# A hybrid decoder layer on one core: mask transfers of the SSD branch issued two groups ahead, with five wide buffers for three, and ScalarE's mask work in unbound halves

## The chip, the cores and the metric

The kernel runs on one core of a Trainium2 chip. A core has a matrix engine (TensorE, PE in the profile, its weight loads PEld), VectorE (DVE), ScalarE (ACT), GpSimd (POOL) and a sync engine (SP). Each engine works off its own instruction list in order; between engines there are semaphores. Transfers run on 16 DMA engines and are issued here from SP (weights) and POOL (masks). The metric is the device time of one execution in microseconds (us); lower is better. What is compared is the median of several executions.

## The reference, cut to what matters

The layer is a SwiGLU feed-forward, a mixer with two branches (Mamba-2 SSD and retention), and a second feed-forward, for 256 tokens of width 1024 in float32. The change touches the SSD branch: 4 groups of 8 heads, two chunks of 128 tokens.

```python
def segsum_exp(a):
    cs = jnp.cumsum(a, axis=-1)
    diff = cs[..., :, None] - cs[..., None, :]
    n = a.shape[-1]
    mask = jnp.tril(jnp.ones((n, n), dtype=bool))
    return jnp.exp(jnp.where(mask, diff, -jnp.inf))
...
    cb = jnp.einsum('bclgn,bcsgn->bgcls', cm, bm)
    scores = cb[:, :, None] * segsum_exp(a)
    y_diag = jnp.einsum('bgrcls,bcsgrp->bclgrp', scores, xdt)
...
    y_off = jnp.einsum('bclgn,cbgrpn,bgrcl->bclgrp', cm, prev_states, jnp.exp(a_cs))
    y = y_diag + y_off + xs * d_skip.reshape(g_, r_)[..., None]
```

`segsum_exp` is the decay mask: for every head a 128 x 128 matrix exp(cs[l] - cs[s]) for s <= l.

## The kernel before

**Weights and PE.** All projections run in split precision. A weight tile comes in by a transfer of 1 MB into `wst` (4 buffers). `half` makes of each half of it a rounded high part `wh` with a cast on ScalarE (L129) and the rest `wl` with a subtraction on VectorE (L130), 4 buffers each. `mm3` (L138 to L140) then runs three matmuls a product: high by high, high by low, low by high. So every weight tile needs two casts and two subtractions ahead of its 48 matmuls, and a late cast stops PE.

**Order of the work.** The mixer's steps are written out by hand in `ORDER`. A scheduler places each engine's instructions at build time: of those whose data it expects to be there, the one that stands first in the program goes first, so that later work can fill gaps. It works with expected times; the chip then runs each engine's list in order and waits where data are late. `tc.issue_after(ins)` binds what is issued inside it to stand behind the instruction `ins` on the same engine. `half` keeps its last cast and its last subtraction for that purpose (`last_hi`, `last_lo`).

**The SSD steps of a group g.** `decays` writes the cumulative sums of the decays to a small tensor `rows` in DRAM. `ml.g` (`mask_rows`) issues on POOL four transfers out of it: for both chunks the 8 heads' rows, broadcast to 128 partitions, into the wide buffers `m` (L645, 512 KB each), and two of 128 KB into `ec` (L648). `masks.g` (`ssd_masks`) does on ScalarE, for each chunk, eight Relus with the head's own sum as bias (L661) and an Exp (L170), then an Exp of `ec`. `bc` makes the score products of all groups, `mul.g` multiplies both masks by them on VectorE (L669), `states.g` scales the inputs (`xd` L626, `xe` L631) and makes the chunk's states on PE (L636), and `back.g` runs PE's products with the masks (L679) and the states (L689), and adds on VectorE (L685, L691, L692). `norma.g`, `normb.g` normalise, `z.g.*` are gate projections (their Silu at L170), `v.*` the retention's values, `bs.g.*` the branch's output projection.

**Buffers.** The wide buffers (tag `m`) are three: one group takes two. The first `m` tiles of the tag go to `dt` and `decays`, and retention later uses the same tag. `ec` has one buffer. In `ORDER`, `ml.g` stands behind `back.(g-1)`, the step that reads the former group's masks. ScalarE also switches its function table (`need`) between Exp ("e") and Silu ("s").

Of the kernel before, what the change touches and what calls it, by code (L numbers as in the profile page):

```python
# [12 lines left out]
F32 = mybir.dt.float32  # L13
F32R = mybir.dt.float32r
I32 = mybir.dt.int32
AF = mybir.ActivationFunctionType
ALU = mybir.AluOpType

P = 128
# [23 lines left out]
STAGE_BUFS = 4  # L43
HALF_BUFS = 4
SLOTS = 17
WIDE_BUFS = 3
F1 = 7

ORDER = (
# [30 lines left out]
def layer(ctx: ExitStack, tc: tile.TileContext, a, out, packing):  # L80
    nc = tc.nc
    pe, act, dve = nc.tensor, nc.scalar, nc.vector
# [10 lines left out]
    def nm(s):  # L93
        uid[0] += 1
        return f"{s}_{uid[0]}"
# [22 lines left out]
              .transpose(1, 0, 2))  # L118
        return st.rearrange("p (k n) -> p k n", k=nk)

    last_lo, last_hi = [None], [None]

    def half(v):
        nk, n = v.shape[1], v.shape[2]
        hi = wp.tile([P, 1024], F32R, tag="wh", name=nm("wh"), bufs=HALF_BUFS)
        lo = wp.tile([P, 1024], F32R, tag="wl", name=nm("wl"), bufs=HALF_BUFS)
        hi = hi[:, :nk * n].rearrange("p (k n) -> p k n", k=nk)
        lo = lo[:, :nk * n].rearrange("p (k n) -> p k n", k=nk)
        last_hi[0] = act.copy(hi, v).ins  # L129
        last_lo[0] = dve.tensor_tensor(lo, v, hi.bitcast(F32), ALU.subtract).ins  # L130
        return hi, lo

    def split_into(hi, lo, src):
# [34 lines left out]
    def lookup(*args, **kw):  # L168
        with tc.issue_after(phase["load"]):
            phase["uses"].append(act.activation(*args, **kw).ins)  # L170
# [89 lines left out]
    def early_project(w, cols, u, at_kt, between):  # L260
        sts = [load(w, 0, KD, c0, 256) for c0 in cols]
        ps = [proj_ps().rearrange("p f t -> p (f t)") for _ in range(2)]
        ps += [misc_ps() for _ in range(2)]
        for kh in range(2):
            hv = [half(st[:, 4 * kh:4 * kh + 4, :]) for st in sts]
            for kk in range(4):
                kt = 4 * kh + kk
                if kt == at_kt:
                    between()
                for i in range(2):  # L270
                    for f in range(2):
                        mm3(ps[2 * i + f][:, :T + 2], at(hv[i], al, kk, slice(f * P, (f + 1) * P)),
                            wide_at(u, kt), kt == 0, kt == KD - 1)
        return ps

    def pair_project(w, c0, u):
        st = load(w, 0, KD, c0, 256)
        ps = proj_ps()
        for f in range(2):
            hv = half(st[:, :, f * P:(f + 1) * P])  # L280
            for kt in range(KD):
                mm3(ps[:, f, :], at(hv, al, kt), at(u, al, kt), kt == 0, kt == KD - 1)
        return ps

    def split_project(w, c0, c1, u):
        st = stage()
        fetch(st, w, lambda m: np.stack([m[:, c:c + P].reshape(KD, P, P) for c in (c0, c1)])
              .transpose(2, 0, 1, 3))
        st = st.rearrange("p (j k n) -> p j k n", j=2, k=KD)
        ps = proj_ps()  # L290
        for f in range(2):
            hv = half(st[:, f])
            for kt in range(KD):
                mm3(ps[:, f, :], at(hv, al, kt), at(u, al, kt), kt == 0, kt == KD - 1)
        return ps
# [183 lines left out]
    with tc.tile_pool(name="mx", bufs=1, reuse_waits="tile") as mx:  # L479
# [6 lines left out]
        def small(shape, tag, bufs=1):  # L486
            return mx.tile(shape, F32, tag=tag, name=nm(tag), bufs=bufs)

        def wide(shape, dt=F32):
            return mx.tile(shape, dt, tag="m", name=nm("m"), bufs=WIDE_BUFS)  # L490

# [25 lines left out]
        def need(t):  # L517
            if now[0] != t:
                now[0] = t
                table(table_of[t])  # L520

        dt, av = small([P, 2, NH], "dt"), small([P, 2, NH], "av")
# [45 lines left out]
        def silu_half(key, c0, p2):  # L568
            need("s")
            if p2 == 0:  # L570
                zs[key] = slot([P, 4, T])
            if key == ("z", 0):
                for f in range(4):
                    lookup(zs[key][:, f, :], first[f][0], AF.Silu, bias=first[f][1])
                return
            ps = pair_project(w_in, c0 + p2 * 256, u)
            lookup(zs[key][:, 2 * p2:2 * p2 + 2, :], ps, AF.Silu)

        bn = small([P, 4, P], "bn")
        cs, dend = small([P, 2, NH], "cs"), small([P, NH], "dend")  # L580
        cbs, states, masks = [], {}, {}
# [56 lines left out]
            states[g] = xd, st  # L638

        def mask_rows(g):  # L640
            ec = small([P, 512], "ec")
            m = [wide([P, 8, P]) for _ in range(2)]
            masks[g] = ec, m
            for c in range(2):
                nc.gpsimd.dma_start(m[c], rows[c:c + 1, 8 * g:8 * g + 8, :].broadcast_to([P, 8, P]))  # L645
            for hh in range(2):
                src = rows[1:2, 8 * g:8 * g + 8, :].rearrange("o (i two) l -> two o i l", two=2)[hh]
                nc.gpsimd.dma_start(ec[hh * 64:hh * 64 + 64, :].rearrange("p (i l) -> p i l", i=4),  # L648
                                    src.broadcast_to([64, 4, P]))

        def ssd_masks(g):
            need("e")
            ec, m = masks[g]
            with tc.issue_after(last_hi[0]):
                mask_decays(g, ec, m)

        def mask_decays(g, ec, m):
            for c in range(2):
                for hl in range(8):
                    hd = 8 * g + hl  # L660
                    act.activation(m[c][:, hl, :], m[c][:, hl, :], AF.Relu,  # L661
                                   bias=cs[:, c, hd:hd + 1], scale=-1.0)
                lookup(m[c], m[c], AF.Exp, scale=-1.0)
            lookup(ec, ec, AF.Exp)

        def mask_scores(g):
            for c in range(2):
                with tc.issue_after(last_lo[0]):
                    dve.tensor_tensor(masks[g][1][c], masks[g][1][c], cbs[0][:, g, c, :].unsqueeze(1).broadcast_to([P, 8, P]), ALU.mult)  # L669

        def ssd_back(g):
            (xd, st), (ec, m) = states.pop(g), masks.pop(g)
# [144 lines left out]
        def ret_norm(hd):  # L817
# [16 lines left out]
            "dt": dt_tile, "conv": conv, "decays": decays, "bc": bc_products,  # L834
            "z": lambda g, p2: silu_half(("z", g), C_Z + g * 512, p2),
            "g": lambda g, p2: silu_half(("g", g), C_G + g * 512, p2),
            "states": ssd_states, "masks": ssd_masks, "ml": mask_rows,
            "mul": mask_scores, "back": ssd_back, "norma": norm_a,
            "normb": norm_b, "v": v_tile, "bs": lambda g, q: branch("s", "w_br_ssd", g, q),
            "br": lambda g, q: branch("r", "w_br_ret", g, q),  # L840
# [29 lines left out]
    with tc.tile_pool(name=nm("fp"), bufs=1, reuse_waits="tile") as fp:  # L870
# [6 lines left out]
        for p2 in range(NF // 2):  # L877
# [14 lines left out]
            if p2 == 5:  # L892
                g = sp.tile([P, KD], F32, tag="g", name=nm("g"), bufs=2)
# [74 lines left out]


# [27 lines left out]
```

## Time and profile before

| | us |
|---|---|
| Median of 3 runs | 876.0 (875.28 to 877.59) |
| The profiled execution | 876.26 |
| Its span, first to last instruction | 874.5 |

The profiled execution had a mean granted TensorE clock of 0.994. The profile's lines give an engine, a line of the kernel, an operation, `out<-in` by the program's names and a count; idle time in front of an instruction is put down to what ended it. In the table by stretches each row has, behind its length, the busy time and instruction count of PE, PEld, DVE, ACT and POOL, then PE's granted clock, the share of the DMA engines in use (which can come out a little over 1) and GB/s. Matmuls are pipelined and their ends are modelled, so a busy PE need not be at its peak. The SSD steps lie between about 225 and 430 us of the span; the conv steps, which come first, end near 302.

### The profile page before, as it was taken

The page shows a single profiled execution, that of the slowest core. Times are in us where ns is not written, and L with a number is a line of the kernel's source. Part 1 is how long each engine was busy: PE and PEld are TensorE (multiplying, and loading weights), DVE is VectorE, ACT ScalarE, POOL GpSimd, SP SyncE. Part 2 cuts the span into 40 slices and gives each one's busy share as a digit, 9 for nine tenths or more (in the row PEclk, how much of TensorE's full clock was granted, in tenths as well). Part 3 has the DMA queues.
Part 4 walks back from the last instruction along what each step waited for, and adds up shares of the span by engine and source line. Part 5 has one row for each costly group of instructions (what it writes and reads, how often), then busy time and mean ns, then how long its engine had stood idle before and what let it go on. Part 6 is the DMA issues. An engine that isn't in the chain of part 4 may idle for free.

```text
span 874.5 us, 16689 instructions
## 1 busy us (share of the span) xinstructions
PE 854.7 (98%) x6982; PEld 836.8 (96%) x6982; DVE 667.7 (76%) x1007; ACT 504.4 (58%) x709; POOL 10.4 (1%) x21
## 2 busy tenths in 40 slices
PE   7999999999999999999999999999999999999996
PEld 5999999999999988899999999999999999999896
DVE  6989788996899768668888687976979985455453
ACT  5455454465766876777564559755558744445342
POOL 0000000000100010100000000000000000000000
PEclk9999999999999999999999999999999999999999
DMA  9968878994575445444657574464464695445521
GB/s 361 413 223 331 299 277 307 346 367 146 214 270 194 145 157 194 172 178 181 206 181 289 211 265 152 168 252 147 169 222 175 262 331 175 184 160 184 189 96 48
DMA packets 30589, 193.24 MB, mean 221 GB/s; under 512 B 3489, under 2 KB 3873, under 8 KB 10802
## 3 DMA queue, kind: packets, MB, share of 16 engines
q1 hardware_dynamic: 28658, 186.47, 58.5%
q0 software_dynamic: 1568, 5.28, 1.9%
q8 instruction: 54, 0.88, 0.4%
q10 hardware_dynamic: 288, 0.44, 0.2%
q14 instruction: 21, 0.17, 0.1%
HBM read 191.09 MB, written 1.08 MB: 220 GB/s over the span
## 4 chain that ended last, share of the span: by engine, by line
PE 89%; DVE 4%; ACT 3%; DMA 2%; issue 1%; SPq 0%; POOL 0%; DVEq 0%; ACTq 0%; POOLq 0%
PE proj L140 27%; PE proj L139 27%; PE proj L138 27%; DVE wl L130 2%; PE misc L138 1%; PE misc L140 1%; PE misc L139 1%; PE misc L679 1%; PE misc L206 1%; DMA ec<-rows 1%; DMA m<-rows 1%; DMA ada<-in_ada_w_dram 1%; ACT wh L129 1%; DVE ada L182 0%; PE misc L689 0%
## 5 line engine op out<-in xcount | busy, mean ns | idle before, releaser
L129 ACT CAST wh<-wst 128x1024 fp32r<-128x1024 f32 (+3 forms) x282 | 289.0, 1032 | 277.6 <-PE proj L139 188.2
L130 DVE TENSOR_TENSOR wl<-wst,wh 128x1024 fp32r<-128x1024 f32 (+3 forms) x282 | 336.6, 1200 | 133.2 <-ACT wh L129 132.9
L138 PE MATMUL proj<-uh,wh 128*128 128x256 f32 (+1 forms) x1336 | 376.9, 283 | 2.3 <-ACT uh L223 2.3
L140 PE MATMUL proj<-uh,wl 128*128 128x256 f32 (+1 forms) x1336 | 377.3, 283 | 0.8 <-DVE wl L130 0.8
L139 PE MATMUL proj<-ul,wh 128*128 128x256 f32 (+1 forms) x1336 | 375.7, 281 | 0.0
L138 PEld LDWEIGHTS proj<-uh,wh 128*128 128x128 f32 x1336 | 251.0, 188 | 3.0 <-ACT uh L223 2.5
L140 PEld LDWEIGHTS proj<-uh,wl 128*128 128x128 f32 x1336 | 252.3, 189 | 1.3 <-DVE wl L130 1.0
L139 PEld LDWEIGHTS proj<-ul,wh 128*128 128x128 f32 x1336 | 252.3, 189 | 0.5 <-issue 0.2
L138 PE MATMUL proj<-s,wh 128*128 128x256 f32 x320 | 90.4, 284 | 0.2 <-ACT s L134 0.2
L140 PE MATMUL proj<-s,wl 128*128 128x256 f32 x320 | 89.6, 281 | 0.0
L139 PE MATMUL proj<-s,wh 128*128 128x256 f32 x320 | 89.3, 280 | 0.0
L182 DVE SCALAR_TENSOR_TENSOR wst<-wst,cb 128x1024 f32<-128x1024 f32 x56 | 67.5, 1221 | 8.7 <-DMA wst<-in_ada_w_dram 8.5
L138 PEld LDWEIGHTS proj<-s,wh 128*128 128x128 f32 x320 | 60.0, 188 | 1.0 <-issue 0.5
L139 PEld LDWEIGHTS proj<-s,wh 128*128 128x128 f32 x320 | 60.2, 188 | 0.4 <-issue 0.2
L140 PEld LDWEIGHTS proj<-s,wl 128*128 128x128 f32 x320 | 60.1, 188 | 0.2 <-issue 0.2
L140 PE MATMUL proj<-ah,wl 128*128 128x256 f32 x176 | 49.1, 279 | 0.0
L138 PE MATMUL proj<-ah,wh 128*128 128x256 f32 x176 | 49.1, 279 | 0.0
L139 PE MATMUL proj<-al,wh 128*128 128x256 f32 x176 | 49.1, 279 | 0.0
L139 PE MATMUL proj<-wl,ah 128*128 128x256 f32 (+1 forms) x132 | 42.1, 319 | 0.0
L140 PE MATMUL proj<-wh,al 128*128 128x256 f32 (+1 forms) x132 | 42.1, 319 | 0.0
L138 PE MATMUL proj<-wh,ah 128*128 128x256 f32 (+1 forms) x132 | 42.1, 319 | 0.0
L162 ACT ACT_TABLE_LOAD x30 | 38.5, 1283 | 1.2 <-PEq L971 0.7
(222 smaller groups left out, 1127.9 us busy)
## 6 DMA issues: line engine op xcount, KB each, us to landing
wst<-in_mix_w_in_dram SPq DMA_DIRECT2D x52, 1024.0 KB, 4.9
wst<-in_ffn_w_in_dram SPq DMA_DIRECT2D x37, 1024.0 KB, 6.1
wst<-in_ada_w_dram SPq DMA_DIRECT2D x28, 1024.0 KB, 5.9
wst<-in_ffn_w_out_dram SPq DMA_DIRECT2D x17, 1024.0 KB, 4.8
ada<-in_ada_w_dram SPq DMA_DIRECT2D x16, 512.0 KB, 12.3
wst<-in_w_br_ssd_dram SPq DMA_DIRECT2D x8, 1024.0 KB, 4.9
wst<-in_w_br_ret_dram SPq DMA_DIRECT2D x8, 1024.0 KB, 4.9
wst<-in_ffn_w_in_dram SPq DMA_DIRECT2D x7, 896.0 KB, 12.9
```

The lines of the kernel that those rows point to most:

```text
L129: last_hi[0] = act.copy(hi, v).ins
L130: last_lo[0] = dve.tensor_tensor(lo, v, hi.bitcast(F32), ALU.subtract).ins
L138: pe.matmul(o, l[0], r[0], start=first, stop=False, skip_group_check=skip)
L139: pe.matmul(o, l[0], r[1], start=False, stop=False, skip_group_check=skip)
L140: pe.matmul(o, l[1], r[0], start=False, stop=last, skip_group_check=skip)
L162: ins = act.preload_act_table_set(name).ins
L182: dve.scalar_tensor_tensor(st[:, i, :], st[:, i, :], 1.0, cb, ALU.mult, ALU.mult, accum_out=raw[:, j, f0 + i:f0 + i + 1])
L206: pe.matmul(ps[:, :T], mean_m[n], s, start=i == 0, stop=i == len(parts) - 1)
L679: pe.matmul(py[hh * 64:hh * 64 + 64, f * T + c * P:f * T + (c + 1) * P], xd[:, c, hl * 64:hl * 64 + 64], m[c][:, hl, :], start=True, stop= ...
```

## The change

The wide buffers go from three to five and `ec` from one buffer to two. `ml.1` stands directly behind `ml.0`, `ml.2` behind `back.0`, `ml.3` behind `back.1`. `masks.g` becomes two steps: `ma.g` (first chunk) and `mb.g` (second chunk and `ec`), and other steps move between them; `mul.g` now stands ahead of `z.g.0`. The bindings of the mask work to the last cast and of the multiplications to the last subtraction are gone. [...]

```diff
-WIDE_BUFS = 3
+WIDE_BUFS = 5
...
-    "dt z.0.0 decays ml.0 conv.8 conv.4 conv.10 conv.0 conv.1 conv.9 conv.2 conv.11 conv.6 conv.7 "
-    "conv.5 conv.3 masks.0 bc v.0 states.0 mul.0 v.1 back.0 ml.1 v.2 v.3 states.1 norma.0 masks.1 "
-    "v.4 normb.0 z.1.0 mul.1 z.1.1 back.1 ml.2 states.2 bs.0.0 norma.1 bs.0.1 masks.2 v.5 normb.1 "
-    "z.2.0 mul.2 z.2.1 v.6 back.2 ml.3 states.3 bs.1.0 norma.2 v.7 masks.3 normb.2 z.3.0 mul.3 "
-    "bs.1.1 z.3.1 back.3 "
+    "dt z.0.0 decays ml.0 ml.1 conv.8 conv.4 conv.10 conv.0 conv.1 conv.9 conv.2 conv.11 conv.6 "
+    "conv.7 conv.5 conv.3 ma.0 bc v.0 mb.0 states.0 mul.0 v.1 back.0 ml.2 v.2 ma.1 v.3 states.1 "
+    "mb.1 norma.0 v.4 normb.0 mul.1 z.1.0 z.1.1 back.1 ml.3 states.2 bs.0.0 ma.2 norma.1 bs.0.1 "
+    "mb.2 v.5 normb.1 mul.2 z.2.0 z.2.1 v.6 back.2 states.3 bs.1.0 ma.3 norma.2 v.7 mb.3 normb.2 "
+    "mul.3 z.3.0 bs.1.1 z.3.1 back.3 "
...
-        last_hi[0] = act.copy(hi, v).ins
-        last_lo[0] = dve.tensor_tensor(lo, v, hi.bitcast(F32), ALU.subtract).ins
+        act.copy(hi, v)
+        dve.tensor_tensor(lo, v, hi.bitcast(F32), ALU.subtract)
...
-            ec = small([P, 512], "ec")
+            ec = small([P, 512], "ec", 2)
...
-        def ssd_masks(g):
+        def ssd_masks(g, c):
             need("e")
             ec, m = masks[g]
-            with tc.issue_after(last_hi[0]):
-                mask_decays(g, ec, m)
-
-        def mask_decays(g, ec, m):
-            for c in range(2):
-                for hl in range(8):
-                    hd = 8 * g + hl
-                    act.activation(m[c][:, hl, :], m[c][:, hl, :], AF.Relu,
-                                   bias=cs[:, c, hd:hd + 1], scale=-1.0)
-                lookup(m[c], m[c], AF.Exp, scale=-1.0)
-            lookup(ec, ec, AF.Exp)
+            for hl in range(8):
+                hd = 8 * g + hl
+                act.activation(m[c][:, hl, :], m[c][:, hl, :], AF.Relu,
+                               bias=cs[:, c, hd:hd + 1], scale=-1.0)
+            lookup(m[c], m[c], AF.Exp, scale=-1.0)
+            if c == 1:
+                lookup(ec, ec, AF.Exp)
...
-                with tc.issue_after(last_lo[0]):
-                    dve.tensor_tensor(masks[g][1][c], masks[g][1][c], cbs[0][:, g, c, :].unsqueeze(1).broadcast_to([P, 8, P]), ALU.mult)
+                dve.tensor_tensor(masks[g][1][c], masks[g][1][c],
+                                  cbs[0][:, g, c, :].unsqueeze(1).broadcast_to([P, 8, P]), ALU.mult)
...
-            "states": ssd_states, "masks": ssd_masks, "ml": mask_rows,
+            "states": ssd_states, "ma": lambda g: ssd_masks(g, 0), "mb": lambda g: ssd_masks(g, 1), "ml": mask_rows,
...
-    nc = bacc.Bacc("TRN2", target_bir_lowering=False, num_devices=1)
+    nc = bacc.Bacc("TRN2", target_bir_lowering=False, num_devices=1,
+                   dynamic_dma_scratch_size=8192)
```

More of the change, by code (lines that the diff above doesn't have):

```diff
@@ L119, in load @@
         return st.rearrange("p (k n) -> p k n", k=nk)
-    last_lo, last_hi = [None], [None]
     def half(v):
```

## The prediction, made before the change was run

> **What bounds the kernel now.** First the page: the span, the busy shares and the chain that ended last.
>
> ```profile
> span 874.5 us, 16689 instructions
> PE 854.7 (98%) x6982; PEld 836.8 (96%) x6982; DVE 667.7 (76%) x1007; ACT 504.4 (58%) x709; POOL 10.4 (1%) x21
> PE 89%; DVE 4%; ACT 3%; DMA 2%; issue 1%; SPq 0%; POOL 0%; DVEq 0%; ACTq 0%; POOLq 0%
> ```
>
> TensorE (PE) is busy for 98% of the span and is 89% of the chain. The change adds and removes no matmul, so it can only win where PE stands still or runs slowly. The table by stretches shows where that is in the SSD stage; the numbers after "PE busy" are us and matmul count, and "PEclk" stands behind the five engines.
>
> ```profile
> 320.00:330.00 10.00, 7.95 (x64) 7.31 (x62) 5.05 (x6) 7.50 (x12) 0.00 (x0) 1.00 0.24 60
> 330.00:340.00 10.00, 8.49 (x65) 7.99 (x66) 8.03 (x11) 5.64 (x8) 0.00 (x0) 1.00 0.54 201
> 360.00:370.00 10.00, 8.48 (x58) 8.08 (x57) 6.74 (x7) 8.13 (x12) 0.00 (x0) 0.83 0.22 70
> 366.50:369.90 3.40, 3.40 (x18) 3.40 (x18) 3.38 (x4) 1.63 (x3) 0.00 (x0) 0.50 0.59 190
> 370.00:373.40 3.40, 3.40 (x30) 3.35 (x29) 2.11 (x3) 1.44 (x2) 0.00 (x0) 1.00 0.99 412
> ```
>
> Idle PE time in the first three rows is 2.05 + 1.51 + 1.52 = 5.08 us. The fourth row is a stretch of 3.4 us at a granted clock of 0.50: 18 matmuls where the next 3.4 us have 30. The timeline of PE names the five stops; the brackets hold the idle time and what ended it.
>
> ```profile
> 326.09 0.38 PE L138 MATMUL proj<-wh,uh 128*128 128x256 f32 x1 [1.03 <-ACT wh L129]
> 327.35 0.39 PE L139 MATMUL proj<-wl,uh 128*128 128x256 f32 x1 [0.88 <-DVE wl L130]
> 327.57 0.28 PE L140 MATMUL proj<-wh,ul 128*128 128x256 f32 x1
> ...
> 331.51 1.10 PE L636 MATMUL misc<-xe,bn 128*128 128x512 f32 x2 [1.65 <-DVE xe L631]
> ...
> 364.38 0.38 PE L138 MATMUL proj<-wh,uh 128*128 128x256 f32 x1 [0.64 <-ACT wh L129]
> 365.64 0.39 PE L139 MATMUL proj<-wl,uh 128*128 128x256 f32 x1 [0.88 <-DVE wl L130]
> ```
>
> The stops belong to head groups 1 and 2. At full clock matmuls start 0.11 us apart (30 in 3.4 us) and each is shown 0.28 long, so every stop also hides up to 0.17 us in which the next would have started: 5 x 0.17, some 0.8 us on top of 5.08. What PE lacks is a weight cast (wh, L129) on ScalarE (ACT) and the subtraction behind it. The timeline of ACT shows why it is late.
>
> ```profile
> 309.23 1.05 ACT L129 CAST wh<-wst 128x1024 fp32r<-128x1024 f32 x1
> 310.17 0.59 ACT L637 COPY st<-misc 128x512 f32<-128x512 f32 x1
> 310.65 2.46 ACT L661 ACTIVATE m<-m,cs 128x128 f32<-128x128 f32 x8
> 313.14 1.06 ACT L170 ACTIVATE m<-m 128x1024 f32<-128x1024 f32 x1
> 317.78 1.58 ACT L661 ACTIVATE m<-m,cs 128x128 f32<-128x128 f32 x5 [3.58 <-DMA m<-rows]
> ...
> 323.53 0.63 ACT L170 ACTIVATE ec<-ec 128x512 f32<-128x512 f32 x1 [1.87 <-DMA ec<-rows]
> 324.06 1.04 ACT L170 ACTIVATE m<-m 128x1024 f32<-128x1024 f32 x1
> 325.01 2.92 ACT L129 CAST wh<-wst 128x1024 fp32r<-128x1024 f32 x3
> ```
>
> The same timeline for group 2, and from ACT's waits between 284 and 410 the row for m (us in total, times, longest).
>
> ```profile
> 357.08 0.99 ACT L661 ACTIVATE m<-m,cs 128x128 f32<-128x128 f32 x3 [2.94 <-DMA m<-rows]
> ...
> 363.29 1.99 ACT L129 CAST wh<-wst 128x1024 fp32r<-128x1024 f32 x2
> ```
>
> ```profile
> ACT m L661 <- DMA m<-rows: 8.8, 3, 3.6
> ```
>
> From 309.23 to 325.01 no cast starts: 15.8 us of mask work, of which 3.58 + 1.87 = 5.45 us is waiting for transfers of m and ec. Group 2 waits 2.94; the third wait of the 8.8 us, 8.8 - 3.58 - 2.94 = 2.3, is group 3's, and it stops PE nowhere. The transfers are late because their buffers are; this is the timeline of GpSimd (POOL), which issues them.
>
> ```profile
> 235.17 1.14 POOL L645 DMA_DIRECT2D m<-rows  x2 [1.52 <-DMA rows<-m]
> 236.29 1.26 POOL L648 DMA_DIRECT2D ec<-rows  x2
> 237.55 0.57 POOL L645 DMA_DIRECT2D m<-rows  x1
> 312.32 1.09 POOL L645 DMA_DIRECT2D m<-rows  x2 [74.21 <-PE misc L679]
> 315.91 1.26 POOL L648 DMA_DIRECT2D ec<-rows  x2 [2.49 <-DVE s L692]
> 350.20 1.12 POOL L645 DMA_DIRECT2D m<-rows  x2 [33.03 <-DVE wl L130]
> ```
>
> **The change part by part.** *More buffers, earlier transfers.* With five m buffers, ml.1 can issue at about 238 both transfers of group 1 and both of its ec; group 1's second half now waits until 312.32 for back.0, its ec until 315.91. Groups 2 and 3 get their last buffers after back.0 and back.1, one group before they are used, so a landing has more than 30 us (350.20 less 315.91). This removes the ACT waits of 5.45, 2.94 and 2.3 us. Take 5.45 us off 325.01 and group 1's first cast starts near 319.6, before PE ran dry (326.09 less 1.03 = 325.06). The subtractions and the xe product, late only behind these casts, move with it. Take 2.94 off 363.29 and it starts at 360.35; cast (1.05) and subtraction (327.35 less 326.09, 1.26) make 2.3 us, so its low half is there at 362.7, before PE ran dry at 364.38 less 0.64 = 363.74. That margin is 1 us; the split below widens it. So all five stops should go: 5.08 + 0.8 = 5.9 us.
>
> The half-clock stretch follows the second pair of stops at once. By the counts it costs 12 of 30 matmuls, 12 x 3.4/30 = 1.4 us; by the clock 3.4 x 0.5 = 1.7. I take 1.5 and let it go with the stops. The first three stops, with more idle time, brought no such stretch, so the link is likely and not certain.
>
> [...]
>
> *What the early transfers collide with.* Between 238 and 256 group 1's remaining 0.5 MB of m and its ec, perhaps another m for group 2, join the weight transfers. These rows price it: the transfers issued from 235 to 239 (count, size, median us to landing), all m transfers, the busiest stretch, and the casts from 240 to 280 (busy us, mean ns, idle time before them).
>
> ```profile
> m<-rows POOLq DMA_DIRECT2D x3, 512.0 KB, 10.2
> wst<-in_mix_w_in_dram SPq DMA_DIRECT2D x1, 1024.0 KB, 10.1
> ```
>
> ```profile
> DMA to landing us min/median/max: 4.8/6.6/13.7
> ```
>
> ```profile
> 240.00:250.00 10.00, 10.00 (x86) 10.00 (x86) 9.13 (x15) 6.79 (x11) 0.00 (x0) 1.00 1.01 358
> ```
>
> ```profile
> L129 ACT CAST wh<-wst 128x1024 fp32r<-128x1024 f32 x15 | 15.7, 1049 | 13.1 <-PE proj L139 13.1
> ```
>
> DMA is full from 240 to 250 and PE still starts 86 matmuls. At 358 GB/s another 0.8 to 1.3 MB takes 2.2 to 3.6 us and is moved into the time behind it. Casts come 40/15 = 2.7 us apart, a weight tile lasts two of them, 5.4 us, and there are four stage buffers; a tile that lands after 10.1 + 3.6 us still comes inside three tiles' 16 us. Cost 0; if that cover were gone, at most the 3.6 us.
>
> *Mask work in halves, unbound.* The same 64 Relus (8 in 2.46 us, so 0.31 each), 8 Exps and 4 ec Exps remain, as do the table loads: the letters asked for by `need` still alternate once per group. Nothing is saved in work; it moves. Without bindings an operation may be put ahead of casts as soon as its data are thought to be there. In the conv stage ACT stands idle before casts for 13.1 of 40 us; the 32 Relus of groups 0 and 1 (9.8 us) fill some 30 us of it. That takes up to 4.9 us of group 1's Relus out of the tight stretch. Each delays a cast by 0.3 us at most; its cover is the cast buffers, three halves of 2.7 us ahead of PE. Cost 0, but see the second rival for waits.
>
> *Multiplications by the scores*, unbound, on VectorE (DVE), as large as the subtraction of 1.26 us: they need the Exp and the score products of bc, after the conv stage where DVE is 9.13 of 10 busy. DVE has room afterwards (5.05 and 8.03 above). Between 0 and one pair, 2.5 us; I take 0, since group 3's equal work stopped nothing. *z after mul, norms between the halves*: the same matmuls in another order, 0 by the same rows. [...] The wider m pool also serves retention, where PE is not short of a buffer in any row above: 0.
>
> *Sum*, against the profiled execution: 876.26 - 5.9 - 1.5 = 868.9 us. It stands 0.26 above the median of 876.0, so the median to expect is 868.6; I leave 0.4 for a small new wait and say **869.0**. What is late next is PE itself.
>
> **The rivals.** *Part of it* (13%): ACT still waits for an m transfer, because an unbound Relu for group 2 or 3 is put right behind its transfer's issue. Then one of the two groups of stops stays, 1.52 + 0.3 with the half-clock stretch's 1.5, or 3.56 + 0.5: 3.3 or 4.1 us remain of the 7.4, so 872 to 872.7, and 871 to 873.4 with the bounds of the stops. For it: the Relu at 317.78 was placed 3.58 us before its data. Against it: such Relus come last in the order and fill gaps.
>
> *Slower* (16%): the same in the conv stage, for groups 0 and 1. There the landings are slow: the second m, issued near 235.7 (median 10.2), lands near 245.9, the third, at 237.55 (13.7), near 251.3, so the next near 256.6. If the Relus of both groups stand at the head of ACT's queue from 240 on, ACT holds its casts for up to 16.6 us. The cover is 3 x 2.7 = 8.1 us less cast and subtraction (2.3), 5.8 us; beyond that point PE stops: 16.6 - 5.8 = 10.8 us, and with 5.9 + 1.5 saved the end is 876.0 + 10.8 - 7.4 = 879.4, with a half-clock stretch or two 881 to 882. It decides at one ACT wait above 5.8 us, or several that add up to it. Against it: the gaps take eight Relus (2.46 us) in some 7.5 us, one m in that time, which is slower than the landings follow each other (5.3). [...]
>
> *No change* (12%): the casts are late for another reason, such as mask work put ahead of them in one block as before (of the 15.8 us without a cast 10.3 are no wait). Then 874 to 877.
>
> *The half-clock stretch stays* (5%): 876.0 - 5.9 = 870.1.
>
> **How the numbers follow.** Forecast 54% (867 to 871), the rivals 13, 16, 12 and 5%. The range 867 to 877 leaves out the slower case and the edges of two others, some 20%. A measurement can tell 0.3%, 2.6 us, from no change: faster (below 873.4) is 54 + 13 + 5 = 72%, within 12%, slower 16%.
>
> **What would show it.** Right: in the stretches 320 to 340 and 360 to 370 PE is 10.00 busy at clock 1.00; ACT's waits for m and ec are gone; POOL issues six to seven mask transfers more or less in a row near 235; no stretch of ACT without casts lasts over 11 us. Wrong: ACT waiting for m between 238 and 262 with PE below 86 matmuls per 10 us there (second rival); an ACT wait for m near 315 or 353 (first); a PE stop ended by DVE's m or ec would be a new bound that I priced at nothing.

## The result, and the profile after

| | before, us | after, us |
|---|---|---|
| Median, 6 runs each | 875.64 (873.07 to 877.59) | **869.7** (868.67 to 870.23) |
| The profiled execution | 876.26 | 870.23 |
| Its span | 874.5 | 868.4 |

The ratio of the times is 0.9934, with a 95% interval of 0.9917 to 0.9952. The forecast was 869.0, in a range of 867 to 877. The page first; its matmul count is the one of before.

```profile
span 868.4 us, 16684 instructions
PE 852.7 (98%) x6982; PEld 835.4 (96%) x6982; DVE 667.0 (77%) x1007; ACT 502.5 (58%) x709; POOL 10.3 (1%) x21
PE 89%; DVE 5%; ACT 3%; DMA 2%; issue 1%; SPq 0%; DVEq 0%; ACTq 0%
```

These shares hardly differ from those of before, and a reader who stopped here would learn nothing: 6 us of 870 don't show in an average. The table by stretches is where they show. The first three rows are from the SSD stage, the next three from the conv steps.

```profile
320.00:330.00 10.00, 8.84 (x71) 8.18 (x70) 7.09 (x9) 7.39 (x17) 0.00 (x0) 1.00 0.48 156
330.00:340.00 10.00, 10.00 (x85) 9.95 (x84) 6.05 (x10) 6.76 (x9) 0.00 (x0) 1.00 0.55 191
360.00:370.00 10.00, 10.00 (x85) 9.95 (x84) 6.47 (x8) 7.62 (x12) 0.00 (x0) 1.00 0.56 210
...
240.00:250.00 10.00, 10.00 (x86) 10.00 (x85) 8.11 (x13) 9.47 (x23) 0.80 (x2) 1.00 1.03 370
250.00:260.00 10.00, 10.00 (x86) 10.00 (x85) 9.12 (x16) 10.00 (x22) 0.00 (x0) 1.00 0.89 298
260.00:270.00 10.00, 10.00 (x86) 10.00 (x85) 9.20 (x16) 10.00 (x24) 0.00 (x0) 1.00 0.53 192
```

Before, the first three stretches had PE busy for 7.95, 8.49 and 8.48 us. In 320 to 330, 1.16 us of idle time is left; the other two are full now, and 360 to 370 has its clock back (0.83 to 1.00). In the conv steps the DMA engines are as full as before (1.03 in 240 to 250, for 1.01) and stay busy longer (0.89 of 250 to 260, for 0.63), ACT has almost no gap left in these three rows (9.47, 10.00 and 10.00 us busy), and PE starts its 86 matmuls in every stretch all the same.

The timeline of POOL shows the transfers where the change put them.

```profile
235.50 1.13 POOL L644 DMA_DIRECT2D m<-rows  x2 [1.53 <-DMA rows<-m]
...
240.23 0.57 POOL L644 DMA_DIRECT2D m<-rows  x1
312.07 1.09 POOL L644 DMA_DIRECT2D m<-rows  x2 [71.27 <-PE misc L674]
```

Nine transfers go out in one row from 235.50 to 240.8, where five did before: between the two m shown first and the one shown last stand, in turn, two ec, two m and two ec. That is all of groups 0 and 1, and the first m of group 2. The next two m have to wait for back.0 and are issued at 312.07: by the order of the steps, the second of group 2 and the first of group 3.

Here is the stop that is left, in the timelines of PE, VectorE and ScalarE. Line numbers have moved by one in the changed kernel: the cast is L128, the subtraction L129.

```profile
328.59 1.10 PE L635 MATMUL misc<-xe,bn 128*128 128x512 f32 x2 [1.17 <-DVE xe L630]
```

```profile
325.42 1.23 DVE L129 TENSOR_TENSOR wl<-wst,wh 128x1024 fp32r<-128x1024 f32 x1 [2.36 <-ACT wh L128]
326.56 1.28 DVE L625 TENSOR_TENSOR s<-misc,dt 128x512 f32<-128x512 f32 x2
327.76 0.68 DVE L630 TENSOR_TENSOR xe<-s,dend 128x512 f32<-128x512 f32 x1
```

```profile
312.55 0.63 ACT L169 ACTIVATE ec<-ec 128x512 f32<-128x512 f32 x1
316.61 1.87 ACT L655 ACTIVATE m<-m,cs 128x128 f32<-128x128 f32 x6 [3.43 <-DVE wl L129]
318.39 1.04 ACT L128 CAST wh<-wst 128x1024 fp32r<-128x1024 f32 x1
...
320.75 1.05 ACT L128 CAST wh<-wst 128x1024 fp32r<-128x1024 f32 x1
321.70 2.75 ACT L655 ACTIVATE m<-m,cs 128x128 f32<-128x128 f32 x9
324.34 1.04 ACT L128 CAST wh<-wst 128x1024 fp32r<-128x1024 f32 x1
```

Read it from PE backwards. PE stops for `xe`. VectorE makes `xe` behind a subtraction that it could not start before 325.42, since the cast at 324.34 was late. In front of that cast stand nine Relus, and further up six more, which ScalarE waited 3.43 us to begin. The waits name a subtraction as what ended that wait, but this is a transfer: the group of DMA issues from 311.5 to 313.5 shows that the two m transfers issued from 312.07 on land after 4.8 us in the median. The first of them took 4.4, so it landed near 316.5, and the Relus began at 316.61.

```profile
m<-rows POOLq DMA_DIRECT2D x2, 512.0 KB, 4.8
```

So sixteen Relus (the last one follows at 325.28), those of group 2's second half and of group 3's first, are placed right behind the issue of their transfers, and the casts that PE needs now stand behind them. Their result is wanted much later: VectorE multiplies group 2's masks from 357.24 on, and PE uses them at 384.30.

### The profile page after: what moved, and what is told of

Its sections match the earlier page's. It is cut to its first block, busy times and chain, and to the rows that moved or that the text cites. A ratio compares the mean times of both kernels' runs of the same rounds, so it can differ in the third digit from the quotient of the medians.

```text
span 868.4 us, 16684 instructions
## 1 busy us (share of the span) xinstructions
PE 852.7 (98%) x6982; PEld 835.4 (96%) x6982; DVE 667.0 (77%) x1007; ACT 502.5 (58%) x709; POOL 10.3 (1%) x21
## 4 chain that ended last, share of the span: by engine, by line
PE 89%; DVE 5%; ACT 3%; DMA 2%; issue 1%; SPq 0%; DVEq 0%; ACTq 0%
PE proj L139 27%; PE proj L138 27%; PE proj L137 27%; DVE wl L129 2%; PE misc L137 1%; PE misc L139 1%; PE misc L138 1%; PE misc L674 1%; DMA wst<-in_ada_w_dram 1%; PE misc L205 1%; ACT wh L128 1%; DVE wst L181 1%; DMA ada<-in_ada_w_dram 1%; DMA wst<-in_ffn_w_out_dram 1%; PE misc L684 1%
## 5 line engine op out<-in xcount | busy, mean ns | idle before, releaser
L128 ACT CAST wh<-wst 128x1024 fp32r<-128x1024 f32 (+3 forms) x282 | 289.3, 1031 | 275.8 <-PE proj L138 185.4
L129 DVE TENSOR_TENSOR wl<-wst,wh 128x1024 fp32r<-128x1024 f32 (+3 forms) x282 | 336.7, 1200 | 135.4 <-ACT wh L128 134.9
L181 DVE SCALAR_TENSOR_TENSOR wst<-wst,cb 128x1024 f32<-128x1024 f32 x56 | 67.4, 1220 | 10.1 <-DMA wst<-in_ada_w_dram 10.0
```

The costliest lines, as they stand in the source:

```text
L181: dve.scalar_tensor_tensor(st[:, i, :], st[:, i, :], 1.0, cb, ALU.mult, ALU.mult, accum_out=raw[:, j, f0 + i:f0 + i + 1])
```

## The experiments

One theory: the earlier transfers carry the gain; the missing bindings carry none of it and cause the stop that is left. Its rival: the missing bindings and the new order matter, because mask work may fill gaps in the conv steps. Each experiment below takes one of the parts alone. The times of before come from the same chips: 874.17 (23 runs) beside the first four, 874.53 (11 runs) beside the next four.

| kernel | m, ec buffers | bindings | median, us (range; runs) | ratio to before, 95% |
|---|---|---|---|---|
| e1_transfers | 5, 2 | as before | 869.05 (867.63 to 870.8; 6) | 0.9933, 0.9918 to 0.9948 |
| e2_unbound | 3, 1 | none | 875.49 (872.51 to 879.05; 12) | 1.0012, 0.9997 to 1.0027 |
| e3_bound | 5, 2 | as before | 868.6 (868.19 to 871.2; 6) | 0.9932, 0.9917 to 0.9947 |
| e4_three | 3, 1 | none | 873.57 (871.63 to 877.16; 12) | 0.9988, 0.9973 to 1.0002 |
| e5_after_again | 5, 2 | none | 869.94 (868.84 to 872.08; 6) | 0.9949, 0.9936 to 0.9962 |
| f1_late_bound | 5, 2 | Relus of groups 2, 3 | 867.75 (867.04 to 868.41; 4) | 0.9921, 0.9908 to 0.9934 |
| e6_four | 4, 2 | as before | 868.9 (867.9 to 870.8; 6) | 0.9936, 0.9924 to 0.9948 |
| e7_four_one | 4, 1 | as before | 870.9 (868.95 to 872.59; 6) | 0.9961, 0.9948 to 0.9974 |

### The transfers alone, on the kernel before

```diff
-WIDE_BUFS = 3
+WIDE_BUFS = 5
...
-    "dt z.0.0 decays ml.0 conv.8 conv.4 conv.10 conv.0 conv.1 conv.9 conv.2 conv.11 conv.6 conv.7 "
+    "dt z.0.0 decays ml.0 ml.1 conv.8 conv.4 conv.10 conv.0 conv.1 conv.9 conv.2 conv.11 conv.6 conv.7 "
...
-            ec = small([P, 512], "ec")
+            ec = small([P, 512], "ec", 2)
...
+                   dynamic_dma_scratch_size=8192)
```

(`ml.2` and `ml.3` move as in the change; the masks stay one bound step. The last line is what the expectations call the smaller scratch; a kernel without it has what they call the default.)

> The kernel before with the early transfers alone: five wide buffers, two ec, the smaller scratch, ml one or two groups earlier; masks in one step, still bound behind casts. Theory A (late transfers make the casts late): PE's stops near 326 to 331 and 364 to 366 go or shrink to under 1.5 us in sum, ACT's waits for m and ec are gone for groups 1 and 2, time 869 to 871, like the changed kernel. Rival B (the mask work stands ahead of the casts as a block, bound to them): one or both groups of stops stay, time 873 to 876.

The whole gain is there, 869.05. PE doesn't stop once between 225 and 460, and ScalarE never waits for m or ec. Two stretches of the SSD stage, then ScalarE's timeline at the place of the first stops:

```profile
320.00:330.00 10.00, 10.00 (x80) 9.37 (x79) 7.72 (x9) 5.22 (x7) 0.00 (x0) 1.00 0.62 206
360.00:370.00 10.00, 10.00 (x85) 9.95 (x84) 8.01 (x9) 6.59 (x10) 0.00 (x0) 1.00 0.55 210
```

```profile
309.99 1.05 ACT L129 CAST wh<-wst 128x1024 fp32r<-128x1024 f32 x1
...
311.42 2.75 ACT L661 ACTIVATE m<-m,cs 128x128 f32<-128x128 f32 x9
...
315.00 2.16 ACT L661 ACTIVATE m<-m,cs 128x128 f32<-128x128 f32 x7
317.06 0.63 ACT L170 ACTIVATE ec<-ec 128x512 f32<-128x512 f32 x1
...
320.06 2.00 ACT L129 CAST wh<-wst 128x1024 fp32r<-128x1024 f32 x2
```

The same block of mask work without a cast, 309.99 to 320.06, only without the waits in it: 10.1 us for 15.8 before. PE has cover for that much. The block needn't be split.

### The bindings alone, on the kernel before

```diff
-            with tc.issue_after(last_hi[0]):
-                mask_decays(g, ec, m)
+            mask_decays(g, ec, m)
...
-                with tc.issue_after(last_lo[0]):
-                    dve.tensor_tensor(masks[g][1][c], masks[g][1][c], cbs[0][:, g, c, :].unsqueeze(1).broadcast_to([P, 8, P]), ALU.mult)
+                dve.tensor_tensor(masks[g][1][c], masks[g][1][c], cbs[0][:, g, c, :].unsqueeze(1).broadcast_to([P, 8, P]), ALU.mult)
```

> The kernel before with the bindings taken away alone: three buffers, transfers as before, masks in one step. Theory A: ACT still waits about 3 us each for group 1's second half, ec and group 2, stops of PE stay in part, time 872 to 876. Rival B: the Relus leave the tight stretch, no stretch without casts is over 11 us, time 869 to 871.

No gain: 1.0012. With the transfers still late, free placement makes ScalarE's waits in front of Relus longer, not shorter: 18 us from 225 to 460 for 8.8 before. One of them in its timeline, then PE's waits from 225 to 460 (us in total, times, longest), then the stretch from 360 to 370.

```profile
312.06 0.59 ACT L637 COPY st<-misc 128x512 f32<-128x512 f32 x1
319.17 2.45 ACT L660 ACTIVATE m<-m,cs 128x128 f32<-128x128 f32 x8 [6.51 <-DVE s L697]
```

```profile
PE misc L636 <- DVE xe L631: 2.1, 2, 1.9
PE proj L139 <- DVE wl L130: 1.7, 2, 0.9
PE proj L138 <- ACT wh L129: 0.6, 1, 0.6
```

```profile
360.00:370.00 10.00, 8.53 (x70) 8.13 (x69) 6.61 (x7) 10.00 (x19) 0.00 (x0) 1.00 0.18 54
```

The last row bears on a question that the prediction had left open. PE is idle in it as long as before (8.53 us busy for 8.48), but it starts 70 matmuls and not 58, at a granted clock of 1.00 and not 0.83. The stops are there and the half-clock stretch isn't.

### The bindings put back, and the buffers taken back, in the changed kernel

```diff
+    last_lo, last_hi = [None], [None]
...
-        act.copy(hi, v)
-        dve.tensor_tensor(lo, v, hi.bitcast(F32), ALU.subtract)
+        last_hi[0] = act.copy(hi, v).ins
+        last_lo[0] = dve.tensor_tensor(lo, v, hi.bitcast(F32), ALU.subtract).ins
...
+            with tc.issue_after(last_hi[0]):
...
+                with tc.issue_after(last_lo[0]):
```

(The first `with` encloses the Relus and Exps of one half, the second the multiplication.)

> The changed kernel with both bindings put back (each half behind the last cast ahead of it, the multiplications behind the last subtraction). Theory A: the gain stays, time 868 to 870.5; and ACT's waits of 3.4 and 3.3 us near 316 and 354 go, since the Relus of groups 2 and 3 come later, with them the one stop of PE left near 328.6 (1.2 us), so that it may be up to 1.3 us faster than the changed kernel. Rival B: the stops come back, 872 to 875.

```diff
-WIDE_BUFS = 5
+WIDE_BUFS = 3
...
-            ec = small([P, 512], "ec", 2)
+            ec = small([P, 512], "ec")
```

> The changed kernel with three wide buffers and one ec: its order, halves and unbound work stay, the early transfers can't. Theory A: ACT waits for group 1's second half and ec again, stops of 2 to 6 us, time 871 to 875. Rival B: no more than 1 us above the changed kernel, 869 to 871.

With the bindings back the time is 868.6, and the stop is gone: no wait of PE between 225 and 460. With the buffers gone the ratio is 0.9988, so halves, order, missing bindings and the smaller scratch together give 0.1% in the median and 0.3% at most by the interval, for 0.7% with the buffers. In that kernel ScalarE waits longer for m from 225 to 460 than before (16.7 us for 8.8), and PE stops at the same kinds of instruction, for 3.8 us in all:

```profile
ACT m L655 <- DMA m<-rows: 16.7, 4, 5.4
```

```profile
PE misc L635 <- DVE xe L630: 1.9, 1, 1.9
PE proj L138 <- DVE wl L129: 1.3, 2, 0.9
PE proj L137 <- ACT wh L128: 0.6, 1, 0.6
```

Its stretch from 360 to 370 also has a clock of 1.00. The rival falls: next to nothing of the gain comes from what it names.

### The one stop that is left

The changed kernel was run again beside a version that binds only the Relus whose transfers are issued late, those of groups 2 and 3; groups 0 and 1 stay free to fill the gaps of the conv steps.

```diff
+    last_hi = [None]
...
-        act.copy(hi, v)
+        last_hi[0] = act.copy(hi, v).ins
...
-            for hl in range(8):
-                hd = 8 * g + hl
-                act.activation(m[c][:, hl, :], m[c][:, hl, :], AF.Relu,
-                               bias=cs[:, c, hd:hd + 1], scale=-1.0)
+            with tc.issue_after(last_hi[0]) if g > 1 else ExitStack():
+                for hl in range(8):
+                    hd = 8 * g + hl
+                    act.activation(m[c][:, hl, :], m[c][:, hl, :], AF.Relu,
+                                   bias=cs[:, c, hd:hd + 1], scale=-1.0)
```

> The changed kernel as it is, beside the three others of this group on one chip. Both theories: 868.5 to 870.5, one stop of PE of 1.2 us near 328.6, waits of ACT for m of 3.4 and 3.3 us near 316 and 354.

> The changed kernel with the Relus of groups 2 and 3 alone bound behind the last cast ahead of them in the program; groups 0 and 1 stay free to fill the conv stage. If the one stop left comes from the Relus that wait near 316 and then stand ahead of two casts: ACT's waits for m go, the stop near 328.6 goes, 867.5 to 869.5, 0.5 to 1.5 us below the changed kernel. If it comes from VectorE's own order (xe behind a subtraction): the stop stays, no difference.

The second profile of the changed kernel has the same stop (1.4 us, again for `xe`). With the binding it is gone, and no mask work stands between the casts there, as ScalarE's timeline shows:

```profile
311.15 0.63 ACT L170 ACTIVATE ec<-ec 128x512 f32<-128x512 f32 x1
315.80 1.05 ACT L129 CAST wh<-wst 128x1024 fp32r<-128x1024 f32 x1 [4.03 <-PE proj L140]
...
318.18 1.04 ACT L129 CAST wh<-wst 128x1024 fp32r<-128x1024 f32 x1
```

ScalarE waits even a little longer than in the changed kernel, 4.03 us for 3.43, but now for a cast buffer that PE frees: the casts are ahead of PE, and this wait costs nothing. The median is 867.75, the lowest of all kernels that were run, 2.2 us below the changed kernel on the same chip, and the two ranges don't overlap. The stop accounts for 1.4 us and the matmul hidden in it; the rest, some 0.6 us, is within the spread of the runs. That it beats e1, e3 and e6, which stop nowhere either, isn't shown: their ranges overlap.

### How many buffers

On e1, four m buffers for five; and then a single ec buffer with the default scratch.

```diff
-WIDE_BUFS = 5
+WIDE_BUFS = 4
```

> The kernel before with the early transfers, but four wide buffers for five; two ec, smaller scratch. By the issue order group 0 and group 1 take all four before 240, groups 2 and 3 each wait for the step back of the group two ahead. If what counts is that a group's transfers are issued one step back earlier: the same time as with five, 868 to 870, no stop over 1 us. If the fifth buffer counts: ACT waits for m in group 2, 870.5 to 873.

```diff
-            ec = small([P, 512], "ec", 2)
+            ec = small([P, 512], "ec")
...
-                   dynamic_dma_scratch_size=8192)
```

> The same with one ec and the default scratch: the smallest early form. ec of group 1 is again issued near 316 and lands 5 to 8 us later. If ec's wait of 1.9 us was part of what held the casts: a wait of ACT for ec of 1 to 4 us, stops up to 2 us, 869 to 872. If m alone counts: 868 to 870.

The fifth m buffer gives nothing that can be measured (868.9 for 869.05). The second ec buffer does: without it ScalarE waits for ec, here in its timeline, and PE stops once, here in its waits. The two intervals only touch, and the scratch was changed along with it; but the waits point to ec.

```profile
321.59 0.64 ACT L170 ACTIVATE ec<-ec 128x512 f32<-128x512 f32 x1 [2.94 <-DMA ec<-rows]
```

```profile
PE misc L636 <- DVE xe L631: 1.9, 1, 1.9
```

So late transfers of 128 KB are the likely cost of 2.0 us (870.9 less 868.9) of a gain of 5.6: the casts stand behind the Exp that waits for them.

### How much cover the casts have

The slower rival said that ScalarE could hold its casts back in the conv steps by 5.8 us before PE stops. To measure this, ten or twenty more copies of 128 x 512 elements go on ScalarE behind a cast of `conv.6`, and the next casts are bound behind them. They compute nothing that is used.

```diff
-        act.copy(hi, v)
+        with tc.issue_after(block[0]) if block[0] else ExitStack():
+            last_hi[0] = act.copy(hi, v).ins
...
+            if p2 == 6:
+                idle = small([P, 512], "idle")
+                for _ in range(10):
+                    with tc.issue_after(block[0] or last_hi[0]):
+                        ins = act.copy(idle, cb[:, :512]).ins
+                    block[0] = ins
```

> The changed kernel with ten more copies of 128 x 512 on ScalarE (0.47 us each, 4.7 us; into a tile that nothing reads) behind the last cast of the seventh conv weight tile in the program's numbering (conv.6), and the casts after it bound behind them. The prediction's cover, 5.8 us of ACT ahead of PE: no stop of PE in the conv stage, time as the changed kernel, 868.5 to 871. A rival with less cover (VectorE at 0.9 can't catch up): stops of 1 to 4 us between 280 and 310.

> The same with twenty copies, 9.4 us. The prediction's cover of 5.8 us: PE stops for 9.4 less 5.8, 3.6 us, plus up to 3 us for the other ACT work that stays in the stretch; time 873 to 877. If the cover is longer than 9.4 us: no stop, 869 to 871. If VectorE can't catch up: 6 to 10 us.

One run each: 870.21 and 877.79, with before at 875.81. The casts around the ten copies, and PE's only wait for a cast from 225 to 460:

```profile
266.30 1.07 ACT L130 CAST wh<-wst 128x1024 fp32r<-128x1024 f32 x1
...
275.83 1.99 ACT L130 CAST wh<-wst 128x1024 fp32r<-128x1024 f32 x2
```

```profile
PE proj L139 <- ACT wh L130: 0.3, 1, 0.3
```

The next cast comes 9.53 us after the last, where 2.7 is the rhythm: 6.8 us late. PE stops for 0.3, with the matmul hidden in it 0.45, so the cover is 6.4 us. With twenty copies:

```profile
265.87 1.05 ACT L130 CAST wh<-wst 128x1024 fp32r<-128x1024 f32 x1
...
283.79 3.88 ACT L130 CAST wh<-wst 128x1024 fp32r<-128x1024 f32 x4
```

```profile
276.22 0.60 PE L593 MATMUL misc<-k,s 128*128 128x128 f32 x4
...
278.44 1.04 PE L632 MATMUL misc<-k,s 128*128 128x128 f32 x8
284.88 0.58 PE L139 MATMUL proj<-uh,wh 128*128 128x256 f32 x1 [5.40 <-ACT wh L130]
```

```profile
283.70:290.60 6.90, 5.26 (x23) 4.96 (x24) 4.63 (x4) 3.97 (x5) 0.00 (x0) 0.51 0.33 99
290.60:297.50 6.90, 6.90 (x60) 6.90 (x60) 3.81 (x5) 3.47 (x4) 0.00 (x0) 1.00 0.58 218
```

Here the cast is 283.79 - 265.87 - 2.7 = 15.2 us late. PE spends 3.3 us of it (276.22 to 279.48) on products that need no cast and stops for 5.40: 15.2 - 3.3 - 5.4 = 6.5, the same cover. And now the half-clock comes. It begins within the stop (the clock of the whole first row is 0.51, that of 274 to 284 still 0.99), and in the 5.7 us that are left of the stretch when the stop ends PE starts 23 matmuls, where the next 6.9 us have 60. The expectation did not have this stretch, and the single run lies 0.8 us above its 873 to 877. So the rival's mechanism exists, the cover was right to about 0.7 us, and the changed kernel stays far from it.

## Why the prediction was right, and where its sum was not

**What bounds the kernel, and the chain that was to be cut: right.** Late m and ec transfers held ScalarE, ScalarE held the casts, PE stopped. Cutting the first link alone (e1) takes all five stops away (5.1 us of idle time); changing anything else without it leaves stops of 4.4 us (e2) and 3.8 us (e4).

**Group 1's first cast near 319.6: right.** It came at 320.06 in e1, which is the kernel that this step described, and at 318.39 in the changed kernel.

**All five stops go: four did, and the fifth shrank from 1.65 us to 1.17.** The step that failed is "a landing has more than 30 us". It took the distance between two groups' issues (350.20 less 315.91) as time that a landing has. What counts on ScalarE, whose casts stood behind the waiting Relu, is where the scheduler placed that Relu, and without the binding it was right behind the issue. So ACT's waits for m did not go: 8.2 us of them are left (4.8 and 3.43), for 8.8 before, though only the 3.43 us lead to a stop of PE. The first rival had this mechanism, and its sign, waits near 315 and 353, came at 316.61 (3.43 us) and 353.84 (3.28 us); its price was whole groups of stops (3.3 to 4.1 us with the half-clock). It occurred at a smaller size: 1.17 us of idle time and 0.17 hidden, 1.3 us. Against the sum of 868.9 the profiled execution took 870.23, which is just that 1.3 more.

**The half-clock stretch, 1.5 us: gone from the profile, but tied too firmly to the stops.** e2 and e4 keep the stops of group 2 and run at a clock of 1.00 from 360 to 370. That one execution of a kernel has such a stretch and another hasn't is shown near the start of the span. There the changed kernel's two profiles have the same stop of 2.32 us in front of a projection, and these are 3.8 us from just before its end on, first in the result's profile, then in e5's:

```profile
17.90:21.70 3.80, 3.49 (x17) 3.49 (x18) 3.80 (x8) 2.40 (x4) 0.00 (x0) 0.57 1.01 412
17.90:21.70 3.80, 3.30 (x25) 3.10 (x26) 3.80 (x8) 2.55 (x4) 0.00 (x0) 1.00 1.01 412
```

The two executions took 870.23 and 868.84. So the stretch of before, too, most likely belonged to that execution rather than to the kernel. Before's times point the same way: in 23 runs they go from 872.63 to 877.42, and the six with a mean clock of 0.998 all lie between 872.63 and 874.12, the one with the lowest clock, 0.992, at 877.38. The base of the sum, 876.26, was therefore some 2 us above the median that more runs gave (874.17 and 874.53), and the sum took 1.5 us off for the stretch: the two cancel. Counted without both it is 874.2 to 874.5 less 5.9, so 868.3 to 868.6, where e3 came out (868.6; e6 868.9, e1 869.05); the residual stop makes 869.6 to 869.9 of it, which is where the changed kernel is. Measured side by side (e5), the change gains 4.6 us (874.53 less 869.94), which is 5.9 less 1.3; the 5.9 us between the medians of the result's table rest on six runs of before that spread over 4.5 us. That the forecast lay within 0.7 us of the median owes something to the cancelling and to the 0.4 us that was left for "a small new wait", in truth 1.3.

**DMA contention, 0: right, though the landings were longer than thought.** Nine mask transfers went out in the row, not "six to seven". The m transfers issued from 235 to 241 took 14.1 us to land in the median (19.6 at most), not 10.2, and no PE stop follows: PE starts its 86 matmuls in each of the three stretches from 240 to 270.

```profile
m<-rows POOLq DMA_DIRECT2D x5, 512.0 KB, 14.1
```

**Unbound Relus fill the conv stage's gaps at no cost: right, and worth nothing.** These are ScalarE's two groups there, 240 to 280 (busy us, mean ns, idle time before them):

```profile
L128 ACT CAST wh<-wst 128x1024 fp32r<-128x1024 f32 x14 | 14.6, 1045 | 2.2 <-PE proj L138 2.2
L655 ACT ACTIVATE m<-m,cs 128x128 f32<-128x128 f32 x40 | 13.3, 399 | 1.5 <-DMA m<-rows 1.5
```

Forty Relus, five halves of eight, went into the 13.1 us that stood idle before. ScalarE waited 1.5 us in all for m, against 6.4 of cover: the second rival didn't occur. But e1, with none of these Relus moved, is no slower; once the transfers were early, ScalarE had room for them later too.

**Multiplications and order, each 0: not contradicted.** f1 has both, and PE waits for nothing in it between 225 and 460. What `dynamic_dma_scratch_size=8192` costs by itself no run shows; e4 has it without the buffers, together with the halves, the order and the missing bindings, at 873.57 beside 874.17 of before.

## What to carry to other kernels

Ask of a transfer not when its result is needed but where the first instruction that touches it was placed: what stands behind that instruction on its engine waits with it (in the changed kernel ScalarE waited 3.43 us in front of Relus whose result VectorE takes 40 us later, and the casts behind them came late for PE, which stopped for 1.17 us), and if urgent work stands there with less cover than the wait, it is paid for. Cut the late transfer with a buffer first, and give the freedom to move work only to instructions whose data were issued long ago; bind those whose transfer has just been issued behind the work that can't wait. A term that rests on one profiled execution, such as a clock stretch, belongs in the range until a second execution shows it.

## What the runs showed of the hardware that was not expected

- **The clock falls in some executions and not in others.** One execution of before had 3.4 us at 0.50 after stops of 0.64 and 0.88 us; e2 and e4 had as much idle time in the same stretch, 360 to 370 (PE 8.53 and 8.50 us busy, for 8.48), and a clock of 1.00. Near 18 us of the span before and the changed kernel have a stop of 2.32 us; over the 3.8 us from 17.90 on the clock is 0.56 in the profile of before, 0.57 in the changed kernel's first and 1.00 in its second. Within and behind one stop of 5.40 us it was 6.9 us at 0.51. What starts the fall no run shows.
- **A landing of 512 KB took from 4.4 us**, for the first of the pair issued at 312.07, **to 19.6**, for the last of nine issued in a row between weight transfers. PE stopped for xe after the short one and nowhere after the long one.
- **What a wait is put down to can be a bystander.** The 3.43 us in the changed kernel stand under a subtraction, the 6.51 us in e2 under a VectorE operation; at both places m transfers had been issued shortly before, from 312.07 and 313.60 on. The first in the changed kernel landed after 4.4 us, and the Relus began 4.54 us after its issue; the two in e2 landed after 5.8 us in the median, and the Relus began 5.57 us after the first one's issue.
